# Chunked attention by pairs of heads in 64-row matmuls, on one core

## The chip, the cores and the metric

The kernel runs on one core of one Trainium2 chip. A core has TensorE (matmuls, written PE in the profile, its weight loads PEld), VectorE (DVE), ScalarE (ACT), GpSimd (POOL) and SyncE (SP), which starts most transfers. Matmuls write into PSUM, eight banks of 512 float32 columns in each of 128 partitions; VectorE and ScalarE read from there. The metric is the device time of one execution in microseconds (us); lower is better.

## The reference

One layer of a streaming encoder over 1024 positions of 1024 features, in float32. Cut to what matters here:

```python
def chunk_attention(q, k, v, rel_bias):      # 8 heads of 64
    # chunks of 64 positions; each attends to its own and the 8 chunks before
    ...
        s = einsum('bqhd,bkhd->bhqk', qb, kb) * scale + bias
        s = where(valid, s, -inf)
        pr = softmax(s, axis=-1)
        return einsum('bhqk,bkhd->bqhd', pr, vb)

def reference(x, p, ...):
    hn = rmsnorm(h, norm_mix_g)
    z = hn @ w_in
    u = z[..., :512]                          # four pooling groups
    q, k, v = split(z[..., 512:], 3)
    a = pool_mixer(u, pool_w, pool_b, pool_scale)
    o = chunk_attention(q, k, v, rel_bias)
    h = h + concatenate([a, o]) @ w_out
    # then a gated MLP with a causal convolution, a gated input embedding, a final norm
    ...
```

## The kernel before

Every large product is made in three matmuls (`mm3`): both operands are split into a high part and a remainder (`split`: a rounding copy on ScalarE, a subtraction on VectorE), and high by high, high by low and low by high are added in PSUM. A step of 128 contraction rows and 512 columns is thus three matmuls of 512 columns.

The stages follow each other: load x and start the first head pair's q and k and the first half of v; attention, with the rest of the input projection dealt out among it; the pooling mixer and the output projection; the MLP; the gate and the final norm. TensorE's order is the order in which the program issues (`manual_schedule`); the other engines are ordered by a scheduler with priorities (`high_priority`) and dependences.

Attention works by tiles of 128 queries. Query tile t needs the key tiles t-4 to t, so 1, 2, 3, 4 or 5 key tiles (`key_tiles`); the eight query tiles of a head need 1, 2, 3, 4, 5, 5, 5, 5. The loop visits i = 0 to 63, eight query tiles for each of eight heads, one head after the other. In a visit:

- `scores(i)`: the operands of a head are stacked in 128 rows (`qk_stack`): `Q1` holds q high over q low, `K2` and `K1` hold k so that two full-row matmuls make all products of high and low parts. Scores go to banks 4 and 5. Then VectorE adds the bias and takes the row maximum (as a minimum of the negated scores) in one instruction (line 354 for five key tiles, 362 for fewer), ScalarE makes the exponential with its row sum (364), VectorE the reciprocal (365), and ScalarE (every third visit, 367) or VectorE (369) scales.
- filling: `credit` steps of the remaining input projection (`rest`, made of `project` and `project_v`), in banks 0 and 1. `fill_room` deals `FILL` steps out over the visits.
- in the middle of the filling, `probs_t(i - 2)`: 128 by 128 transposes (378) of the probabilities of two visits ago into banks 6 and 7, with the high copy (385) and the low part (386) into `PT`.
- at every second visit `values`: the products with V (395, 396), 256 queries at a time, in bank 2 or 3, and their sum over the high and low columns (401, 402) into `o32`.

There are three buffers `Sb` of probabilities and two of bias. Evacuations of filling products are on lines 272 (q and k), 268 (v) and 454 (pooling groups).

Of the kernel before, what the change touches and what calls it, by code (L numbers as in the profile page):

```python
# [11 lines left out]
P = 128  # L12
# [52 lines left out]
FILL = 164  # L65
BASE = 2.0
LATER = 3
DRAIN = 4
# [4 lines left out]
def key_tiles(i):  # L73

    return min(i % NTOK + 1, BANDT) if 0 <= i < N_HEADS * NTOK else 0


def fill_room():


    vec_t, pe_t = [], []
    for i in range(N_HEADS * NTOK):
        a, b = key_tiles(i), key_tiles(i - 2)
        vec_t.append(BASE + 0.2 * key_tiles(i - 3) + 0.13 * b)
        pe_t.append(0.11 * a + 0.11 * b + (0.22 * (key_tiles(i - 5) + 1) if i % 2 and i >= 5 else 0.0))
    lo, hi = 0.0, 10.0
    for _ in range(60):
        m = (lo + hi) / 2
        room = [max(0.0, m * v - p) / 0.65 for v, p in zip(vec_t, pe_t)]
        lo, hi = (m, hi) if sum(room) < FILL else (lo, m)  # L90
    return room


def trunk(tc, xT, pT, vecs, w_qk0, w_in, w_v, bias, counts, pool_w, w_out, w_up, w_down,
# [4 lines left out]
    with tc.tile_pool(name="sb", bufs=1) as sb, \  # L99
# [47 lines left out]
        st = [small[:, 56 + 3 * i:59 + 3 * i] for i in range(3)]  # L147
        sa = [small[:, b:b + 3] for b in (24, 27, 30, 33, 66, 69)]
# [7 lines left out]
        stacks = []  # L156
        for s in range(2):
            base = r(96 + 12 * s, 3072).rearrange("p (a t) -> p a t", a=3)
            stacks.append((base[:, 0], base[:, 1], base[:, 2]))
# [6 lines left out]
        biasb = [f(12 + 2.5 * s, 640) for s in range(2)]  # L166
        Sb = [f(b, 640) for b in (17, 19.5, 57.5)]
# [106 lines left out]
        def qk_stack(j):  # L274

            Q1, K1, K2 = stacks[j]
            a = slice(HD * j, HD * j + HD)
            b = slice(HD * (1 - j), HD * (1 - j) + HD)
            q, k = qk32[0], qk32[1]
            todo = []  # L280
            for h in range(2):
                z = slice(h * 512, (h + 1) * 512)
                todo += [
                    lambda z=z: act.activation(Q1[a, z], q[a, z], AF.Copy, scale=-0.125),
                    lambda z=z: dve.scalar_tensor_tensor(Q1[b, z], q[a, z], -0.125, rv(Q1[a, z]),
                                                         ALU.mult, ALU.subtract),
                    lambda z=z: act.activation(K2[a, z], k[a, z], AF.Copy),
                    lambda z=z: dve.tensor_tensor(K2[b, z], k[a, z], rv(K2[a, z]), ALU.subtract),
                    lambda z=z: act.activation(K1[b, z], k[a, z], AF.Copy),
                    lambda z=z: dve.tensor_copy(K1[a, z], rv(K2[b, z])),  # L290
                ]
            return todo
# [27 lines left out]
        later += qk_stack(0)  # L320
        run_later(len(later))
        later += qk_stack(1)
# [6 lines left out]
        def load_bias(h):  # L329
            b = biasb[h % 2]  # L330
# [5 lines left out]
        def keys(i):  # L336
            t = i % NTOK
            k0 = max(0, t - 4)
            return i // NTOK, t, k0, t + 1 - k0

        def scores(i):
            h, t, k0, nk = keys(i)
            Q1, K1, K2 = stacks[h % 2]
            b = biasb[h % 2]
            q = Q1[:, t * P:(t + 1) * P]
            S = Sb[i % 3]
            s_ = st[i % 3]
            n, ki = nk * P, k0 * P
            if nk == BANDT:
                for z in range(2):  # L350
                    ks = slice(ki + 320 * z, ki + 320 * z + 320)
                    pe.matmul(PS[:, 4 + z, 0:320], q, K2[:, ks], start=True, stop=False)  # L352
                    pe.matmul(PS[:, 4 + z, 0:320], q, K1[:, ks], start=False, stop=True)  # L353
                dve.tensor_tensor_reduce(
                    S.rearrange("p (a b) -> p a b", a=2), PS[:, 4:6, 0:320],
                    b.rearrange("p (a b) -> p a b", a=2), 1.0, BIG, ALU.add, ALU.min, s_[:, 0:1])
            else:
                nn = max(n, 256)
                z = 4 + t % 2
                pe.matmul(PS[:, z, 0:nn], q, K2[:, ki:ki + nn], start=True, stop=False)  # L360
                pe.matmul(PS[:, z, 0:nn], q, K1[:, ki:ki + nn], start=False, stop=True)  # L361
                dve.tensor_tensor_reduce(S[:, 0:n], PS[:, z, 0:n], b[:, 640 - n:640],  # L362
                                         1.0, BIG, ALU.add, ALU.min, s_[:, 0:1])
            act.activation(S[:, 0:n], S[:, 0:n], AF.Exp, bias=s_[:, 0:1], scale=-1.0, accum_out=s_[:, 1:2])  # L364
            dve.reciprocal(s_[:, 2:3], s_[:, 1:2])
            if i % 3 == 0:
                act.activation(S[:, 0:n], S[:, 0:n], AF.Copy, scale=s_[:, 2:3])
            else:
                dve.tensor_scalar(S[:, 0:n], S[:, 0:n], s_[:, 2:3], None, ALU.mult)

        def probs_t(i):
            h, t, k0, nk = keys(i)
            S = Sb[i % 3]
            w = i // 2
            pt = PT[w % 2]
            pst = PS[:, 6:8].rearrange("p a b -> p (a b)")[:, 0:nk * P]
            for j in range(nk):
                pe.transpose(pst[:, j * P:(j + 1) * P], S[:, j * P:(j + 1) * P], ident)  # L378
            pst = pst.rearrange("p (k q) -> p k q", k=nk)
            i0 = k0 - (t // 2 * 2 - 4)  # L380
            qs = slice(t % 2 * P, (t % 2 + 1) * P)
            hi = pt[:, 0, i0:i0 + nk, qs]
            lo = pt[:, 1, i0:i0 + nk, qs]
            with tc.high_priority(AHEAD):
                act.activation(hi, pst, AF.Copy)
                dve.tensor_tensor(lo, pst, rv(hi), ALU.subtract)

        def values(wi):
            h, w = wi // 4, wi % 4
            pt = PT[wi % 2]  # L390
            ks = list(range(max(0, 2 * w - 4), 2 * w + 2))
            O = PS[:, 2 + wi % 2, 0:256]
            for n_, k in enumerate(ks):
                idx = k - (2 * w - 4)
                pe.matmul(O, V[:, k, h], pt[:, 0, idx], start=n_ == 0, stop=False)  # L395
                pe.matmul(O, V[:, k, h], pt[:, 1, idx], start=False, stop=n_ == len(ks) - 1)  # L396
            j = h % 2
            a = slice(HD * j, HD * j + HD)
            c = slice(HD * (1 - j), HD * (1 - j) + HD)
            with tc.high_priority(AHEAD):  # L400
                act.activation(otmp[a], O[c], AF.Copy)
                dve.tensor_tensor(o32[a, h // 2, w * 256:(w + 1) * 256], O[a], otmp[a], ALU.add)

        nw = [0]
        bankn = [0]

        def project(ct, evac, heads=0, eng=dve):
            hi, lo = wring[nw[0] % 2]
# [913 lines left out]
```

## Time and profile before

| What | us |
|---|---|
| median of 3 runs (lowest, highest) | 1135.18 (1134.28, 1135.48) |
| profiled execution | 1134.33 |
| its span in the trace | 1132.6 |
| TensorE busy in the span | 1123.2 |
| VectorE busy | 889.3 |
| ScalarE busy | 600.6 |
| attention stage, from the first scores to the last values | 54 to 274 |

The profile is of one execution. A row of the group view gives line, engine, operation, output and inputs, shapes and count, then busy time, the mean of one in ns, and the idle time before the group with what ended it. The timeline gives start, length, engine and line. Matmuls overlap, and the length of one is partly modelled; the distance from one start to the next says what it costs TensorE. In the view of stretches the columns are the length, then each engine's busy time with its number of instructions, the granted TensorE clock (1.00 is full), the DMA share and the rate. A row of the waits says who waited for whom, for how long in all, how often, and the longest.

### The profile page before, as it was taken

To read this page: it belongs to the slowest core of one execution; us is meant where nothing else is said; L and a number is where in the kernel's file an instruction comes from. 1 tells how busy PE (TensorE), PEld (TensorE's weight loads), DVE (VectorE), ACT (ScalarE), POOL (GpSimd) and SP (SyncE) were. 2 spreads that over 40 slices of the span, in tenths; PEclk is the share of its full clock that TensorE was granted. 3 is DMA by queue.
4 is the path that set the end of the run, shared out by engine and by line. 5 is a ranking of instruction groups with operands and counts; after the bars stand their busy time and mean duration, and the time that the engine had idled before them with its cause. 6 is when DMAs were issued, how large, how long until landed. Compare 5 with 4: busy or idle time off the path is not lost.

```text
span 1132.6 us, 15484 instructions
## 1 busy us (share of the span) xinstructions
PE 1123.2 (99%) x5554; PEld 948.4 (84%) x5554; DVE 889.3 (79%) x1532; ACT 600.6 (53%) x1056; POOL 143.1 (13%) x188
## 2 busy tenths in 40 slices
PE   9999999999999999999999999999999999999997
PEld 7988998888888888888888888888888888888887
DVE  8678878879658888887788788877877789986845
ACT  8568677765654554444444344444444435564634
POOL 0000000074002210120112011201120112000000
PEclk9999999999999999999999999999999999999999
DMA  7010102104500154575557555765576556420003
GB/s 268 38 49 31 50 12 69 40 29 137 189 19 10 61 148 135 142 174 141 145 153 176 140 143 152 162 157 132 152 160 158 144 149 128 151 93 19 1 27 122
DMA packets 64588, 124.81 MB, mean 110 GB/s; under 512 B 7296, under 2 KB 8704, under 8 KB 64512
## 3 DMA queue, kind: packets, MB, share of 16 engines
q1 hardware_dynamic: 50400, 98.33, 25.9%
q0 software_dynamic: 13824, 25.17, 13.9%
q8 instruction: 43, 0.70, 0.2%
q10 hardware_dynamic: 288, 0.33, 0.1%
q14 instruction: 33, 0.27, 0.1%
HBM read 109.13 MB, written 14.68 MB: 109 GB/s over the span
## 4 chain that ended last, share of the span: by engine, by line
PE 91%; DVE 4%; ACT 2%; issue 1%; POOL 1%; DMA 0%; SPq 0%; POOLq 0%; DVEq 0%; ACTq 0%
PE PS L128 28%; PE PS L129 28%; PE PS L130 28%; PE PS L378 2%; PE PS L396 1%; PE PS L395 1%; DVE R L134 1%; PE PS L353 1%; PE PS L352 1%; ACT R L133 0%; PE PS L361 0%; PE PS L360 0%; ACT F L364 0%; DMA F<-in_xT 0%; POOL TB L786 0%
## 5 line engine op out<-in xcount | busy, mean ns | idle before, releaser
L128 PE MATMUL PS<-R 128*128 128x512 f32 (+1 forms) x1136 | 435.1, 383 | 0.0
L130 PE MATMUL PS<-R 128*128 128x512 f32 (+1 forms) x1136 | 430.6, 379 | 0.0
L129 PE MATMUL PS<-R 128*128 128x512 f32 (+1 forms) x1072 | 412.7, 385 | 0.2 <-DVE R L241 0.2
L130 PEld LDWEIGHTS PS<-R 128*128 128x128 f32 x1136 | 213.5, 188 | 40.7
L128 PEld LDWEIGHTS PS<-R 128*128 128x128 f32 x1136 | 213.7, 188 | 38.8 <-ACT R L133 0.5
L133 ACT ACTIVATE R<-F 128x512 fp32r<-128x512 f32 (+2 forms) x225 | 140.6, 637 | 176.2 <-PE PS L129 77.9
L129 PEld LDWEIGHTS PS<-R 128*128 128x128 f32 x1072 | 201.6, 188 | 38.5 <-DVE R L241 1.3
L134 DVE TENSOR_TENSOR R<-F,R 128x512 fp32r<-128x512 f32 (+2 forms) x221 | 152.3, 700 | 46.7 <-ACT R L133 45.5
L1021 DVE TENSOR_TENSOR F<-F,PS 128x512 f32<-128x512 f32 x140 | 92.6, 681 | 6.8 <-PE PS L130 6.6
L133 ACT ACTIVATE BQ<-RW 128x512 fp32r<-128x512 f32 x90 | 52.6, 622 | 81.6 <-PE PS L129 77.6
L711 DVE TENSOR_TENSOR F<-F 128x512 f32<-128x512 f32 x88 | 60.5, 688 | 37.4 <-DMA F<-in_w_up 36.1
L964 POOL DMA_DIRECT2D RW<-Yd x56 | 49.1, 878 | 255.4 <-DMA RW<-Yd 194.5
L964 POOL DMA_DIRECT2D RW<-in_w_down x40 | 35.5, 949 | 236.3 <-DMA RW<-in_w_down 193.9
L134 DVE TENSOR_TENSOR BQ<-RW,BQ 128x512 fp32r<-128x512 f32 x90 | 59.1, 684 | 2.9 <-PE PS L129 2.2
L364 ACT ACTIVATE F<-F,small 128x640 f32<-128x640 f32 (+2 forms) x64 | 44.4, 693 | 21.5 <-DVE small L362 13.4
L129 PE MATMUL PS<-BQ 128*128 128x512 f32 x140 | 54.6, 390 | 0.1
L130 PE MATMUL PS<-BQ 128*128 128x512 f32 x140 | 54.5, 389 | 0.0
L128 PE MATMUL PS<-R,BQ 128*128 128x512 f32 x140 | 54.5, 389 | 0.0
L129 PE MATMUL PS<-R,BQ 128*128 128x512 f32 x140 | 54.5, 389 | 0.0
L130 PE MATMUL PS<-R,BQ 128*128 128x512 f32 x140 | 54.5, 389 | 0.0
L128 PE MATMUL PS<-BQ 128*128 128x512 f32 x140 | 54.5, 389 | 0.0
L847 ACT ACTIVATE F<-F,vec 128x1024 f32<-128x1024 f32 (+1 forms) x25 | 28.6, 1143 | 43.5 <-DVE F L822 37.2
(188 smaller groups left out, 1797.7 us busy)
## 6 DMA issues: line engine op xcount, KB each, us to landing
F<-in_w_up SPq DMA_DIRECT2D x91, 256.0 KB, 3.8
RW<-Yd SPq DMA_DIRECT2D x60, 256.0 KB, 3.6
RW<-Yd POOLq DMA_DIRECT2D x56, 256.0 KB, 4.7
RW<-in_w_down SPq DMA_DIRECT2D x50, 256.0 KB, 2.9
RW<-in_w_down POOLq DMA_DIRECT2D x40, 256.0 KB, 6.2
Yd<-F SPq DMA_DIRECT2D x40, 256.0 KB, 3.5
F<-in_w_in SPq DMA_DIRECT2D x10, 512.0 KB, 3.5
F<-in_xT SPq DMA_DIRECT2D x16, 256.0 KB, 5.8
```

The lines of the kernel that those rows point to most:

```text
L128: pe.matmul(ps, ahi, bhi, start=first, stop=False, skip_group_check=more)
L129: pe.matmul(ps, ahi, blo, start=False, stop=False, skip_group_check=more)
L130: pe.matmul(ps, alo, bhi, start=False, stop=last, skip_group_check=more)
L133: both = (act.activation(hi, src, AF.Copy), dve.tensor_tensor(lo, src, rv(hi), ALU.subtract))
L134: dve.tensor_tensor(lo, src, rv(hi), ALU.subtract))
L352: pe.matmul(PS[:, 4 + z, 0:320], q, K2[:, ks], start=True, stop=False)
L364: act.activation(S[:, 0:n], S[:, 0:n], AF.Exp, bias=s_[:, 0:1], scale=-1.0, accum_out=s_[:, 1:2])
L378: pe.transpose(pst[:, j * P:(j + 1) * P], S[:, j * P:(j + 1) * P], ident)
L711: return dve.tensor_tensor(rawu[to], rawu[a], rawu[b], op)
L847: act.activation(y, Gb[:, 2 + a:2 + b], AF.Identity, bias=vec[:, C_CB + fi:C_CB + fi + 1], scale=cw(2))
L964: pool.dma_start(t, src, accum_op=ALU.add)
L1021: dve.tensor_tensor(t, t, PS[:, 4 + d], ALU.subtract if n in (1, 5) else ALU.add)
```

## The change

Two heads are handled together, each in 64 of TensorE's 128 rows. A *unit* is a pair of heads and a query tile (the two shortest tiles, 0 and 1, make one unit): 28 units, seven for each of four pairs, take the place of 64 visits.

- Operands: q high, q low, k high and k low of the pair lie in tiles of their own, the first head in rows 0 to 63 and the second in rows 64 to 127 (`lay` takes the place of `qk_stack`, with copies of 128 rows). q has one buffer and k two.
- `scores(u)`: three products of 64 rows per key range (high by high, high by low, low by high), alternating between the two heads; the heads write different banks of 4 to 7.
- `probs_t(u - 1)`: each 128 by 128 block is transposed in two halves of 64 rows and 64 columns, which alternate between row halves and write two banks. They are issued first in unit u, right ahead of its scores, so that all 64-row work of a unit is together. For units of five key tiles the first three key tiles go to columns 320 and on of banks 4 to 7, the others to banks 2 and 3.
- `probs_out`: the high copies and low parts, now in two pieces of three and up to two key tiles; `softmax`: as before, with the first head scaled on VectorE and the second on ScalarE. There are two `Sb`, one for each head, and three bias buffers.
- After that the filling steps of the unit, and last `values(u - 1)`, if its tile is odd, for both heads, into the one of banks 0 and 1 that the filling product in progress does not use; if that product has only begun, filling goes on first.
- Filling: `fill_room` has other costs and deals out 168 steps by the new lengths; `project` loads and splits the next block's weights while the present block runs; k comes ahead of q, and `lay_due` says when each half of them may be laid.

```diff
-FILL = 164
-BASE = 2.0
-LATER = 3
-DRAIN = 4
+FILL = 168
+BASE = 6.0
+LATER = 8
+DRAIN = 9
...
+UNITS = [(c, ts) for c in range(N_HEADS // 2) for ts in [(0, 1)] + [(t,) for t in range(2, NTOK)]]
...
+    for u in range(NU):
+        vec_t.append(BASE + 0.2 * (key_tiles(u) + key_tiles(u - 1)) + 0.25 * window_keys(u - 1))
+        pe_t.append(0.4 + 0.18 * key_tiles(u) + 0.11 * key_tiles(u - 1) + 0.48 * window_keys(u - 1))
...
-        room = [max(0.0, m * v - p) / 0.65 for v, p in zip(vec_t, pe_t)]
+        room = [max(0.0, m * v - p) / 0.68 for v, p in zip(vec_t, pe_t)]
...
+        Q = [r(96 + 4 * x, 1024) for x in range(2)]
+        K = [[r(104 + 8 * s + 4 * x, 1024) for x in range(2)] for s in range(2)]
...
+        def scores(u):
...
+                wide = n // 2 if nk > 3 else max(n, 256)
+                places = [[4 + x + 2 * (z + y) for y in range(2 if nk > 3 else 1)] for x in range(2)]
+                for i, (q, k) in enumerate(((Q[0], Kh), (Q[0], Kl), (Q[1], Kh))):
+                    for y in range(len(places[0])):
+                        for x in range(2):
+                            pe.matmul(PS[:, places[x][y], 0:wide], q[halves[x], t * P:(t + 1) * P],
+                                      k[halves[x], ki + y * wide:ki + (y + 1) * wide], start=i == 0, stop=i == 2,
+                                      tile_position=(HD * x, 0))
...
+        def probs_t(u):
...
+                return (4 + 2 * x, 320 + HD * m) if m < 3 else (2, P * x + HD * (m - 3))
...
+                    for y in range(2):
+                        pe.transpose(PS[:, bank + y, col:col + HD], Sb[x][halves[y], m * P:(m + 1) * P],
+                                     ident[halves[y], halves[y]], tile_position=(HD * y, 0))
...
+        def values(u):
...
+            while c_ >= 2 and len(v_ready) < 2 * w + 2 or u < NU - 1 and at[0] < 2:
+                next(fill)
+                credit -= 1
...
+                O = PS[:, (bankn[0] + 1) % 2, 256 * j:256 * j + 256]
...
+        for u in range(NU + 1):
...
+            turned_ = probs_t(u - 1) if u else []
+            sums = scores(u) if u < NU else []
+            probs_out(turned_)
+            for todo in sums:
+                softmax(*todo)
+            if u < NU:
...
+                credit += room[u]
+                while credit >= 1 and next(fill, True) is not False:
+                    credit -= 1
+                    lay_due(u)
+                run_later(LATER)
+                if u:
+                    values(u - 1)
+        for _ in range(DRAIN):
+            next(fill)
+        values(NU - 1)
```

More of the change, by code (lines that the diff above doesn't have):

```diff
@@ L146, in trunk @@
         rstd_tok = small[:, 8:16]
[L147 to L148 removed]
+        st = [small[:, b:b + 3] for b in (24, 27, 30, 33, 56, 59, 62, 66)]
         cnt = small[:, 40:56]
@@ L334, in load_bias, with softmax @@
             pool.memset(b[64:128, 0:64], BIG)
[L336 to L353, printed above, removed]
+        def softmax(x, b, ps, S, s_):
+            n = S.shape[-1]
+            if len(ps.shape) == 3:
@@ L371, in probs_t @@
[L371 to L386, printed above, removed]
@@ L388, in values @@
-        def values(wi):
-            h, w = wi // 4, wi % 4
-            pt = PT[wi % 2]
-            ks = list(range(max(0, 2 * w - 4), 2 * w + 2))
[L392 to L402, printed above, removed]
+            if x:
+                act.activation(S, S, AF.Copy, scale=s_[:, 2:3])
+            else:
+                dve.tensor_scalar(S, S, s_[:, 2:3], None, ALU.mult)
```

225 lines of the change are left out of this document (127 added, 98 removed).

## The prediction

> **What bounds the kernel now.** I read the page first.
>
> ```profile
> span 1132.6 us, 15484 instructions
> PE 1123.2 (99%) x5554; PEld 948.4 (84%) x5554; DVE 889.3 (79%) x1532; ACT 600.6 (53%) x1056; POOL 143.1 (13%) x188
> PE 91%; DVE 4%; ACT 2%; issue 1%; POOL 1%; DMA 0%; SPq 0%; POOLq 0%; DVEq 0%; ACTq 0%
> ```
>
> TensorE is busy all the time and carries the chain that ended last. The change touches only the attention stage, from the first scores at 54 us to the last values at 274 us, so next came the stretch view and the waits of that stage.
>
> ```profile
> core 0: us, PE busy (x) PEld busy (x) DVE busy (x) ACT busy (x) POOL busy (x), PEclk, DMA share, GB/s
> 54.00:274.00 220.00, 219.03 (x1367) 193.93 (x1366) 177.76 (x433) 153.38 (x328) 34.91 (x62) 1.00 0.14 46
> ```
>
> ```profile
> PE PS L378 <- DVE B L386: 0.8, 2, 0.5
> ```
>
> TensorE idles 1.0 us of 220 and its only named wait in the stage is 0.8 us, at a full granted clock. So the stage is as long as its sum of matmul slots. VectorE is busy 177.8 us (81%): if TensorE gets less work, VectorE's order is next. A busy share does not give slots, since matmuls overlap; slots are the distances between starts in the timeline.
>
> ```profile
> 201.14 0.30 PE L352 MATMUL PS<-R 128*128 128x320 f32 x1
> 201.28 0.31 PE L353 MATMUL PS<-R 128*128 128x320 f32 x1
> 201.42 0.31 PE L352 MATMUL PS<-R 128*128 128x320 f32 x1
> 201.57 0.31 PE L353 MATMUL PS<-R 128*128 128x320 f32 x1
> 201.72 0.39 PE L128 MATMUL PS<-R,B 128*128 128x512 f32 x1
> ```
>
> ```profile
> 263.03 0.39 PE L130 MATMUL PS<-R 128*128 128x512 f32 x1
> 263.26 0.71 PE L378 MATMUL PS<-ident,F 128*128 128x128 f32 x5
> 263.72 0.48 PE L128 MATMUL PS<-R 128*128 128x512 f32 x1
> 264.04 0.39 PE L129 MATMUL PS<-R 128*128 128x512 f32 x1
> ...
> 268.50 0.28 PE L395 MATMUL PS<-B,R 128*128 128x256 f32 x1
> 268.61 0.28 PE L396 MATMUL PS<-B,R 128*128 128x256 f32 x1
> ```
>
> A score product of 320 columns takes a slot of 0.145 us (0.58 over four), one of 512 columns 0.23, one of 256 columns 0.12; 384 columns lie between, 0.175. Five transposes with what they push back: from 263.26 to the next product's start, less its 0.23 slot (264.04 - 0.23 = 263.81), 0.55, so 0.11 each. A filling step (three products of 512) takes 0.69.
>
> **Part 1: scores.** Before, a head and query tile multiplies stacked 128-row operands: two products per key range. A head has four tiles of five key tiles (four slots of 320 columns) and tiles of 1, 2, 3, 4 key tiles (two slots of 256, 256, 384, 512): 16 x 0.145 + 4 x 0.12 + 2 x 0.175 + 2 x 0.23 = 3.61 us, for eight heads 28.9. After, three products of 64 rows per range, for two heads in two row halves. If two halves run side by side, a pair of heads has 24 slots of 0.145, 6 + 6 of 0.12 and 3 of 0.175: 5.45 us, for four pairs 21.8. That removes 7.1. One after the other they take 43.6 and add 14.7. No instruction of this trace uses part of the rows, so this is the first open price. I take side by side: the halves read different rows and write different banks.
>
> **Part 2: transposes.** 240 of 0.11 make 26.4 us; the count is in this row.
>
> ```profile
> L378 PE MATMUL PS<-ident,F 128*128 128x128 f32 x240 | 37.1, 274 | 1.0 <-DVE B L386 0.8
> L395 PE MATMUL PS<-B,R 128*128 128x256 f32 x144 | 36.1, 284 | 0.0
> ...
> L378 PEld LDWEIGHTS PS<-ident,F 128*128 128x128 f32 x240 | 28.8, 140 | 9.8 <-DVE B L386 4.3
> L395 PEld LDWEIGHTS PS<-B,R 128*128 128x128 f32 x144 | 27.2, 189 | 1.0
> ```
>
> After, there are 480 of 64 rows and 64 columns, in 240 pairs. Does a pair take half of 0.11? A 128-column transpose lasts as long as a 256-column product (274 and 284 ns) while its weight load is shorter (140 against 189): it looks bound by its columns, and half of them take half. Then 13.2 us remain, 13.2 less. Against it stand products with a single column, which still take 0.10 each:
>
> ```profile
> 334.82 0.79 PE PS L628 x8
> 335.61 0.35 PE PS L128
> ```
>
> If loading the weights sets the slot, a pair takes 0.11 still and nothing is gained; if the halves follow each other, 480 x 0.11 = 52.8, 26.4 more. I take the half, being nearest to the transposes' own rows.
>
> **Part 3: entering and leaving 64-row work.** 28 units (seven per pair of heads) each go in and out once. Going from product to transposes costs nothing today (0.23 from 263.03 to 263.26), so the low end is 0. The high end is a full stop: the tail of a product beyond its slot, 0.39 - 0.23 = 0.16, plus a load of 0.19, so 0.35 each, 19.6 in all. I take 0.2 each, the middle, 0.4 per unit: 11.2 us.
>
> The Trainium skill, "TensorEngine Tiling (Array Packing)", Key Properties, speaks against the change here: changing the tiling mode, not merely the tile, drains TensorE. It gives no price; by it the low end falls away, and the sum below keeps its 11.2.
>
> Values stay at the 288 matmuls of before (two rows of 144): 0. They now write the bank that the next filling product wants, which must wait for two copies and two adds:
>
> ```profile
> L402 DVE TENSOR_TENSOR F<-PS,F 64x256 f32<-64x256 f32 x31 | 13.0, 419 | 2.3 <-ACT F L401 1.9
> ...
> L401 ACT ACTIVATE F<-PS 64x256 f32<-64x256 f32 x31 | 11.7, 378 | 7.9 <-PE PS L396 7.4
> ```
>
> That is 2 x 0.80 = 1.6, behind the next unit's transposes, scores and switches (1.8): 0, and 1.6 for the one window in eight that ends with a product if that cover is late. Fewer, wider splits of q and k, a third bias buffer (one more DMA at the start, ahead of the first filling weights, while value tiles still run) and weights split earlier relieve engines that do not bound: 0. Filling work is the same, only dealt out anew.
>
> **Part 4: the softmax loop.** Before, probabilities are transposed two visits after their scores, in the middle of filling work. After, a unit's transposes stand first in the next unit, and TensorE, being in order, holds all filling products behind them. The loop from transposes to transposes for a unit of five key tiles:
>
> ```profile
> L386 DVE TENSOR_TENSOR B<-PS,B 128x384 fp32r<-128x384 f32 x8 | 4.4, 554 | 1.9 <-ACT B L385 1.7
> L386 DVE TENSOR_TENSOR B<-PS,B 128x256 fp32r<-128x256 f32 x8 | 3.4, 423 | 0.2
> L354 DVE CUSTOM_DVE_ANT_0 F<-PS,F 128x640 f32<-128x640 f32 x32 | 26.1, 816 | 2.6 <-PE PS L353 2.3
> L369 DVE TENSOR_SCALAR F<-F,small 128x640 f32<-128x640 f32 x21 | 12.2, 583 | 0.5
> L365 DVE RECIPROCAL small<-small 128x1 f32<-128x1 f32 x64 | 10.3, 161 | 16.5 <-ACT F L364 16.1
> L272 DVE TENSOR_TENSOR F<-PS,F 128x512 f32<-128x512 f32 x12 | 8.2, 685 | 0.6 <-PE PS L130 0.5
> ```
>
> ```profile
> L385 ACT ACTIVATE B<-PS 128x384 fp32r<-128x384 f32 x8 | 3.9, 485 | 4.7 <-PE PS L378 4.7
> L364 ACT ACTIVATE F<-F,small 128x640 f32<-128x640 f32 x32 | 26.5, 827 | 7.7 <-DVE small L354 6.7 <-DVE small L365 0.9
> L364 ACT ACTIVATION_READ_ACCUMULATOR F<-F,small 128x1 f32 x64 | 12.0, 187 | 0.0
> L367 ACT ACTIVATE F<-F,small 128x640 f32<-128x640 f32 x11 | 9.0, 821 | 0.5 <-DVE small L365 0.5
> ```
>
> Time 0 is the end of the transposes. Scores take 6 x 0.145 + 0.16 = 1.03. The high copies of the first three key tiles lie in the scores' banks and I let them wait: ScalarE has them done at 1.5 and 2.0 (0.485 each). VectorE's low parts (0.55, 0.55, 0.42) end at 3.0, the two additions with bias (0.82 and 0.9 with its accumulator's read) at 3.9 and 4.8. ScalarE's exponentials (0.83 + 0.19) end at 4.95 and 6.0, the second reciprocal at 6.2, its scaling on ScalarE (0.82) at 7.0; five pairs of transposes (0.055) close the loop at 7.3, with handovers 7.4.
>
> TensorE's own work in a unit: transposes 0.55, scores 0.87, switches 0.4, filling by `fill_room` as the diff gives it (7.0 steps at query tiles 5 and 7, 5.3 at tile 4, 4.6 at tile 6, of 0.69), values 16 or 24 x 0.12 at tiles 4 and 6. That is 6.65 at tiles 5 and 7, 7.4 at tile 4, 7.9 at tile 6. So tiles 5 and 7 wait 0.75 each, 8 units, 6.0 us. Units with fewer key tiles have shorter loops and wait nothing.
>
> **Sum.** -7.1 - 13.2 + 11.2 + 6.0, and the 1.0 us of today's idle: -4.1. The profiled execution took 1134.33 us (span 1132.6), 0.85 below the median of 1135.18; from the median, 1131.1.
>
> **The rivals.**
>
> *Copies need not wait* for scores in the same bank: then they run under the scores, the loop is about 1 us shorter, tiles 5 and 7 wait nothing, and the sum is -10.1: 1125; with switches at half price -15.7: 1119.5. In today's trace transposes (banks 6 and 7) and scores (4 and 5) lie apart, so it tells nothing. The Trainium skill, "PSUM — Partial Sum Buffer", section on bank collisions, says two engines must be kept apart in a bank even at different columns; by it this rival falls.
>
> *Other vector work inside the loop* (the other side). VectorE also evacuates filling products (0.685, L272) and splits weights; these are 0.685 long and cannot be interrupted. One such step inside the loop of each unit of five key tiles adds 0.69 at tiles 5, 7 and 4 (12 units) and 0.2 at tile 6 (4): 9.1, a sum of +5.0: 1140. It decides from 0.35 us per unit on (4.1 over 12 units). For it: VectorE is 81% busy and had two visits of slack, now one unit. Against: VectorE has 1 us free at the loop's end, and qk splits shrink.
>
> *Pairs overlap only in part.* Transposes bound by loads: 13.2 lost, tiles 5 and 7 then wait 0.5: +7.1, so 1142. With score slots at 0.19 too, 6.6 more: 1149. The Trainium skill, "TensorE: Matmul & The Clock Gate", measured speedup, has 3.07 of an ideal 4 for four row tiles; no run here shows it.
>
> *The halves do not run side by side*: +14.7 + 26.4 + 11.2 - 1.0 = 51: 1186. Nothing in the trace speaks for it but the missing evidence.
>
> *Nothing changes*: price and gain cancel within 0.2% (2.3 us, about what a measurement of this kernel can tell from no change).
>
> **How the numbers follow.** Forecast case 0.45 (0.30 faster, 0.10 the same, 0.05 slower, as switches cost 0.15 or 0.3), copies free 0.13, vector work in the loop 0.22, partial overlap 0.10, no overlap 0.06, cancelling 0.04. Faster 0.43, same 0.14, slower 0.43. The range leaves out no overlap, the far part of partial overlap and a little at the low end: 1120 to 1147; the forecast's own range is 1127 to 1136.
>
> **What would show it.** Score pairs 0.145 us apart, not 0.29; transposes in pairs 0.055 apart, not 0.11; a gap of about 0.2 us at each change between 64-row and 128-row work; TensorE waiting for the scaling of the second head at the units of tiles 5 and 7 by some 0.75 us, 6 us in the stage. The prediction is wrong if these waits exceed 10 us, or if no slot shrinks.

## The result and the profile after

| | us, median | ratio to before, 95% interval |
|---|---|---|
| before | 1135.12 | |
| with the change | 1162.65 (1162.09 to 1164.92) | 1.0247 [1.023, 1.0265] |

The change makes the kernel 27.5 us slower: the forecast of 1131.1 missed, on the other side and outside its range of 1120 to 1147. The first lines and the chain that ended last, from the page of the kernel after:

```profile
span 1160.8 us, 16207 instructions
PE 1123.4 (97%) x5914; PEld 938.6 (81%) x5914; DVE 868.7 (75%) x1530; ACT 591.6 (51%) x1074; POOL 144.2 (12%) x188
PE 82%; DVE 8%; ACT 5%; issue 2%; DMA 1%; POOL 1%; SPq 0%; POOLq 0%; DVEq 0%; ACTq 0%
```

The span grew by 28.2 us and VectorE's share of the chain from 4 to 8%. Where: the view of stretches, attention first and then all that follows; and TensorE's waits in the first stretch.

```profile
54.00:315.00 261.00, 232.22 (x1786) 195.00 (x1784) 175.78 (x462) 154.75 (x364) 35.51 (x60) 0.99 0.14 48
315.00:1160.00 845.00, 838.78 (x3812) 697.49 (x3810) 657.24 (x1010) 401.89 (x653) 105.20 (x112) 1.00 0.46 122
```

```profile
PE PS L433 <- DVE F L438: 20.0, 16, 2.2
PE PS L395 <- ACT F L351: 4.2, 8, 1.2
PE PS L433 <- DVE R L275: 1.7, 2, 1.0
PE PS L395 <- DVE F L353: 1.7, 4, 0.8
```

TensorE idles 28.8 of the 261 us (before, 1.0 of 220). Nothing is lost after the stage: its last 845 us hold 838.78 us of TensorE work, the amount of before. The first row is the largest part of the answer: 16 times, the products of probabilities with V (line 433) wait for an addition on VectorE (line 438), 20.0 us in all. The transposes (395) wait 5.9 us for the scaling of the softmax, close to the 6.0 of the forecast; seven of the eight waits for the second head's scaling (351) stand behind units of tiles 5 and 7, as forecast. The groups of TensorE's instructions say the same, in their last column:

```profile
L433 PE MATMUL PS<-B,R 128*128 128x256 f32 x144 | 38.8, 302 | 21.8 <-DVE F L438 20.0 <-DVE R L275 1.7
L395 PE MATMUL PS<-ident,F 64*128 64x64 f32 x480 | 22.7, 231 | 5.8 <-ACT F L351 4.2 <-DVE F L353 1.7
```

One such place in the timeline, of TensorE, then of ScalarE and VectorE:

```profile
199.25 0.28 PE L434 MATMUL PS<-B,R 128*128 128x256 f32 x1
200.45 0.39 PE L433 MATMUL PS<-B,R 128*128 128x256 f32 x1 [0.92 <-DVE F L438]
```

```profile
199.57 0.38 ACT L437 ACTIVATE F<-PS 64x256 f32<-64x256 f32 x1
```

```profile
198.66 0.69 DVE L291 TENSOR_TENSOR R<-F,R 128x512 fp32r<-128x512 f32 x1
199.27 0.55 DVE L353 TENSOR_SCALAR F<-F,small 128x640 f32<-128x640 f32 x1
199.73 0.16 DVE L349 RECIPROCAL small<-small 128x1 f32<-128x1 f32 x1
199.98 0.42 DVE L438 TENSOR_TENSOR F<-PS,F 64x256 f32<-64x256 f32 x1
```

The first head's last product starts at 199.25. Its copy (437) and its addition (438) read the left half of a bank; the second head's first product writes the right half of the same bank. It starts at 200.45, right after the addition, instead of at 199.37. The code issues copy and addition inside the loop over the two heads, ahead of the second head's products, and the dependence goes by banks. The Trainium skill, "PSUM — Partial Sum Buffer", section "PSUM bank collisions raise a hardware error", says that a second engine must stay out of a bank even at other columns, on the same 32 partitions; the trace agrees in so far as the program waits in each of the 16 windows.

A long wait can cost a second time, as this view of stretches shows for the one that ends at 114.7 us:

```profile
112.00:114.60 2.60, 0.50 (x5) 0.29 (x3) 1.51 (x4) 2.52 (x6) 0.00 (x0) 0.98 0.00 0
114.60:118.00 3.40, 3.27 (x20) 3.05 (x22) 0.07 (x1) 0.31 (x1) 0.00 (x0) 0.51 0.00 0
118.00:121.00 3.00, 3.00 (x26) 2.37 (x23) 2.61 (x9) 1.63 (x6) 0.00 (x0) 1.00 0.00 0
```

For 3.4 us the granted clock is 0.51, and the value products take slots of 0.21 us in place of 0.12. The same follows the wait of 1.68 us that ends at 184.8 (granted clock 0.50 from 186.2 to 189.6), but not the one of 2.20 us that ends at 276.5 (1.00 from 276.6 to 280.0). Two such stretches, 6.8 us at half clock, cost some 3.4 us.

### The profile page after: what moved, and what is told of

The parts are those of the page before. It is cut to its first block, busy times and chain, and to the rows that moved or that the text cites. A ratio compares the mean times of both kernels' runs of the same rounds, so it can differ in the third digit from the quotient of the medians.

```text
span 1160.8 us, 16207 instructions
## 1 busy us (share of the span) xinstructions
PE 1123.4 (97%) x5914; PEld 938.6 (81%) x5914; DVE 868.7 (75%) x1530; ACT 591.6 (51%) x1074; POOL 144.2 (12%) x188
## 4 chain that ended last, share of the span: by engine, by line
PE 82%; DVE 8%; ACT 5%; issue 2%; DMA 1%; POOL 1%; SPq 0%; POOLq 0%; DVEq 0%; ACTq 0%
PE PS L138 26%; PE PS L139 26%; PE PS L140 25%; DVE B L414 2%; PE PS L433 2%; DVE R L144 2%; PE PS L434 1%; PE PS L395 1%; DVE F L343 1%; ACT B L413 1%; ACT F L348 1%; PE PS L370 1%; ACT R L143 1%; DVE F L438 1%; ACT F L351 1%
## 5 line engine op out<-in xcount | busy, mean ns | idle before, releaser
L143 ACT ACTIVATE R<-F 128x512 fp32r<-128x512 f32 (+2 forms) x235 | 147.2, 637 | 179.0 <-PE PS L139 74.0
L144 DVE TENSOR_TENSOR R<-F,R 128x512 fp32r<-128x512 f32 (+2 forms) x231 | 159.8, 702 | 50.9 <-ACT R L143 44.4
L414 DVE TENSOR_TENSOR B<-PS,B 128x384 fp32r<-128x384 f32 (+2 forms) x104 | 45.1, 463 | 28.7 <-ACT B L413 27.8
L433 PE MATMUL PS<-B,R 128*128 128x256 f32 x144 | 38.8, 302 | 21.8 <-DVE F L438 20.0
L348 ACT ACTIVATE F<-F,small 128x640 f32<-128x640 f32 (+4 forms) x64 | 44.1, 691 | 28.7 <-DVE small L343 23.1
L140 PE MATMUL PS<-R,BQ 128*128 128x512 f32 x140 | 54.5, 389 | 0.0
L139 PE MATMUL PS<-R,BQ 128*128 128x512 f32 x140 | 54.5, 389 | 0.0
```

Source lines behind the costliest of these rows:

```text
L139: pe.matmul(ps, ahi, blo, start=False, stop=False, skip_group_check=more)
L140: pe.matmul(ps, alo, bhi, start=False, stop=last, skip_group_check=more)
L143: both = (act.activation(hi, src, AF.Copy), dve.tensor_tensor(lo, src, rv(hi), ALU.subtract))
L144: dve.tensor_tensor(lo, src, rv(hi), ALU.subtract))
L348: act.activation(S, S, AF.Exp, bias=s_[:, 0:1], scale=-1.0, accum_out=s_[:, 1:2])
L414: dve.tensor_tensor(lo, src, rv(hi), ALU.subtract)
```

## The experiments

Times are medians against the kernel before on the same chip (1135.0 to 1135.8 in all of them). Waits are TensorE's between 54 and 315 us. Line numbers are those of each run's own kernel: the transposes stand in 395 or 398, a filling step begins at 138, the additions that empty the values' bank are 438, 440 or 443.

| Run | us | ratio, 95% interval |
|---|---|---|
| e4, rows in turn | 1169.4 | 1.0308 [1.0293, 1.0324] |
| e2, two banks | 1152.4 | 1.0157 [1.0141, 1.0173] |
| e1, copies after both heads | 1146.8 | 1.0113 [1.0094, 1.0132] |
| e5, e1 and filling dealt anew | 1152.2 | 1.0147 [1.013, 1.0164] |
| e9, e1 without the second scaling | 1140.2 | 1.0042 [1.0025, 1.0059] |
| e6, e1 and softmax first | 1145.6 | 1.009 [1.0075, 1.0105] |
| e7, e1 and values early in a product | 1157.8 | 1.0189 [1.0161, 1.0217] |
| e8, e6 with e7 | 1155.5 | 1.0169 [1.0147, 1.0191] |
| e10, e6 with the loop cut | 1144.0 | 1.0072 [1.0055, 1.0089] |
| e11, e6 levelled | 1145.2 | 1.0085 [1.007, 1.01] |
| e12, e11 and scaling on VectorE | 1144.4 | 1.0078 [1.006, 1.0096] |
| e13, e12 and copies first | 1144.9 | 1.0092 [1.0066, 1.0118] |
| e14, e10 without the values' copies | 1134.7 | 0.9994 [0.9985, 1.0004] |
| e15, e1 two units deep | 1141.0 | 1.0052 [1.0038, 1.0066] |
| e19, e1 and values in banks of their own | 1142.2 | 1.0062 [1.005, 1.0075] |
| e16, e15 with e19 | 1130.2 | 0.9959 [0.9947, 0.9972] |
| e17, e16 and softmax first | 1130.5 | 0.9958 [0.9946, 0.9971] |
| e18, e16 with whole transposes | 1133.9 | 0.9991 [0.9982, 1.0] |

### The values' bank, and the row halves

**e1_out_after** issues both heads' products before either head is copied out.

```diff
-                with tc.high_priority(AHEAD):
-                    act.activation(otmp[a], O[c], AF.Copy)
-                    ...
+                outs_.append((O, halves[j], halves[1 - j]))
+            for O, a, c in outs_:
+                with tc.high_priority(AHEAD):
+                    act.activation(otmp[a], O[c], AF.Copy)
+                    ...
```

> The changed kernel with one edit: in a window of values the products of both heads are issued first, and the two copies and additions that empty their bank after both. Theory (one bank): the second head's products wait in 16 windows for VectorE's addition of the first head, since both heads write halves of one bank; 22.8 us of TensorE's idle time in the changed kernel stand there, 1.08 at the least in each window. Then that wait is gone; the shorter units give some 3 us back to the wait for the softmax, so 1143, 1140 to 1148. Rival (late vectors): the second head would wait anyway, for probabilities or for VectorE's turn; the wait moves and the time stays at 1160 to 1163. Rival (64-row price): most of the loss is in changes of mode and pairs that overlap in part; the wait goes but the time falls by under 8 us, to 1155 or more.

1146.8: 15.9 us less, as expected. The wait between the heads is gone. Its waits:

```profile
PE PS L395 <- ACT F L351: 4.9, 8, 1.0
PE PS L138 <- DVE F L440: 4.1, 4, 2.0
PE PS L395 <- DVE F L353: 3.5, 5, 1.0
```

The transposes now wait 8.4 us, since the stops between the heads no longer give the softmax time, and the next filling product (138) waits 4.1 for the values' bank.

**e2_two_banks** leaves the copies where they were and gives each head a bank (`O = PS[:, 2 + j, 256:512]`).

> The changed kernel with one edit: the first head's values go to columns 256 to 511 of bank 2 and the second head's to those of bank 3, in place of the two halves of the free filling bank; the copies and additions stay behind each head's products. Theory (one bank): the second head no longer waits (0 of 16 windows against 16), but the next unit's transposes, which write banks 2 and 3 for key tiles 4 and 5 and in short units, now wait for the additions, about 1 us in most of 14 windows; 1150, 1145 to 1157. Rival (late vectors): the second head waits as before and the time is 1160 or more.

1152.4. The second head waits no more, but the next unit's transposes do, for the same addition, since they write those banks:

```profile
PE PS L395 <- DVE F L438: 13.4, 23, 1.1
```

Both runs show the shared bank, emptied between the two heads, to be the cause of most of the loss; e2 shows that another bank alone hands the wait on.

**e4_rows_in_turn** issues all scores of one head, then all of the other (`for x in range(2)` as the outer loop), as a test of the row halves in the kernel after.

> The changed kernel with one edit: the score products of a query tile are issued head by head (all of the first 64 rows, then all of the second), not alternating. Theory (pairs run side by side because they alternate): slots of 0.145 us each, not two in one; 12 in place of 6 in a unit of five key tiles, 0.87 us more in 16 units, 0.36 to 0.72 in 12, so 20 us of TensorE work, of which units that wait for the softmax or the bank hide up to 7: 1176, 1170 to 1184. Rival (64-row price): the pairs barely overlap now, so the order does not matter: 1160 to 1166.

1169.4, 6.7 more than the change: below the expected 1170 to 1184 and above the rival's 1166. The halves overlap in part even so. The kernel after first, then e4, in the timeline: transposes, twelve score products, the next product:

```profile
159.98 1.13 PE L370 MATMUL PS<-R 64*128 64x320 f32 x12
161.03 0.39 PE L138 MATMUL PS<-R 128*128 128x256 f32 x1
```

```profile
162.09 1.52 PE L370 MATMUL PS<-R 64*128 64x320 f32 x12
163.55 0.39 PE L138 MATMUL PS<-R 128*128 128x256 f32 x1
```

From the first score to the product 1.05 us became 1.46; with no overlap it would have been near 1.9. That two halves run side by side is shown.

### The waits that are left, one at a time

All of these start from e1.

**e9_no_second_scale** leaves out the scaling of the second head (`if not x:`, only the first scaled), so every second head's output is not normalised.

> The first run's kernel (both heads' products, then the copies) without the scaling of the second head's probabilities by its reciprocal: that ScalarE instruction of 0.81 us (five key tiles) is left out, so the values of every second head are not normalised. TensorE's work is the same. Theory (softmax loop): in eight units TensorE waits 1.2 us for the second head's scaling, 9.4 us in all; the loop gets 0.8 to 0.9 us shorter where it binds, so 5 to 7 us of that wait go: 1140.5, 1139 to 1143. Rival (vector engines' sum of work): ScalarE is at 51% of the span and has time to spare, so leaving out 20 us of its work changes nothing: 1145 to 1148.

1140.2, as expected. The wait at the transposes fell from 8.4 to 3.3, so the softmax's length is what they wait for.

**e5_new_deal** deals the filling by the measured loop lengths and holds values back only right at a product's first step.

```diff
-        vec_t.append(BASE + 0.2 * (key_tiles(u) + key_tiles(u - 1)) + 0.25 * window_keys(u - 1))
+        vec_t.append({0: 7.3, 2: 5.1, 3: 6.0}.get(UNITS[u][1][0], 7.6))
...
-            ... or u < NU - 1 and at[0] < 2:
+            ... or u < NU - 1 and at[0] < 1:
```

> The edit of the first run (both heads' products, then the copies) with the filling steps dealt out anew: unit lengths proportional to 7.6 us for five key tiles, 6.0 for four, 5.1 for three, 7.3 for the unit of two tiles, in place of the formula, and values held back only while the filling product in progress is in its first step, not its first two. Theory (softmax loop of 7.4 us): TensorE's waits at the transposes, 6.7 us in the changed kernel, shrink to 2 or 3; 1136 to 1141, 3 to 5 under the first run. Rival (late vectors): the vector engines set the pace whatever the deal; within 2 us of the first run.

1152.2, a miss. The transposes wait 4.4 instead of 8.4, but one wait for the values' bank is 6.4 us long: VectorE stood behind an operation of the next stage that waited 6.3 us for GpSimd, and ScalarE behind one that waited 6.8.

```profile
PE PS L138 <- DVE F L440: 6.4, 1, 6.4
```

**e6_softmax_first** puts the softmax under `high_priority(AHEAD)`. **e7_values_early** lets values only start while the filling product is at its steps 2 to 5 (`not 2 <= at[0] <= 5`). **e8_all_three** has both and keeps V one tile further ahead (`len(v_ready) < min(2 * w + 3, NTOK)`).

> The first run's kernel with the softmax instructions given the same raised priority as the copies behind transposes and products, so that weight splits, splits of q and k and evacuations are not put among them. Theory (softmax loop with other vector work in it): in a binding unit two foreign VectorE instructions of 0.68 us stand inside the loop (an evacuation of q, a split); with most of them behind it the wait at the transposes falls from 9.4 to about 4 us: 1142, 1139 to 1145. Rival (the loop is its own chain): foreign work only fills its gaps; within 2 us of 1146.8.

> The first run's kernel, with values let in only while the filling product in progress is in its steps 2 to 5 (before: from 2 on), so that at least two filling steps (1.4 us) lie between the values and the next product, which wants their bank. Theory (one bank, second half): the first run's four waits of products for VectorE's addition of values, 4.1 us, go; the added filling steps shift some 2 us to the units after: 1144, 1142 to 1146. Rival: the waits are those of a late VectorE and reappear elsewhere: 1146 to 1149.

> The edits of the two runs before it together, and values of the third and fourth pair held back until one more tile of V is done than they need (2.0 us of waits for the last part of V in the first run). By the theories 9.4 falls to 4, 4.1 and 2.0 to under 1: 1138, 1135 to 1142. If the vector engines only shift their delay, 1144 or more.

e6 gave 1.2 us, which its runs (1143.9 to 1147.2) hardly tell from e1's (1146.1 to 1150.8), though the transposes' waits fell from 8.4 to 5.5. e7 lost 11 against e1 and e8 10 against e6: the wait for the bank fell from 4.1 to 0.9, but the steps taken early to reach the right place were missing in the next unit, which is one of the long ones (of tile 7's filling 3 steps were left in the unit at 213.2, against 7 in e1's at 207.3). e7's waits:

```profile
PE PS L395 <- DVE F L353: 9.5, 7, 2.9
PE PS L395 <- ACT F L351: 5.9, 9, 1.2
```

Much of the loss is the clock: behind waits of 2.2, 2.9 and 1.7 us, e7's profile has 17.1 us at a granted clock of 0.50, some 8.5 us of work lost, where e1's has 3.4 us (1.7).

**e11_level** takes e6 and moves 0.8 steps from tiles 2 and 3 to 5 and 7; **e12_level_dve** scales the second head on VectorE besides; **e13_empty_first** raises the values' copies to `high_priority(4 * AHEAD)` as well.

> The kernel of raised softmax priority with 0.8 filling steps more in the units of query tiles 5 and 7 and 0.8 less in those of tiles 2 and 3, nothing else dealt anew. Theory (softmax loop): tiles 5 and 7 wait some 0.7 us each and have 0.55 more work now; tiles 2 and 3 have shorter loops and wait nothing: waits at the transposes from 6.3 to 3, so 1142.5, 1141 to 1145. Rival (late vectors): no change within 1.5 us, or slower as in the new deal.

> The levelled kernel with the second head's probabilities scaled on VectorE like the first's (0.58 us in place of 0.82 on ScalarE, and one handover less). Theory (softmax loop): the loop is 0.3 to 0.5 us shorter where it binds: 1 to 3 us under the levelled kernel: 1140.5, 1139 to 1143. Rival (VectorE's sum of work): VectorE gets 15 us more and delays evacuations: equal or slower than the levelled kernel.

> The levelled kernel with both heads scaled on VectorE, and the copies and additions that empty the values' bank raised four times as far in priority (240 instructions ahead, not 60). Theory (one bank, second half): the filling product that follows waits for that bank because VectorE does splits and evacuations first (3.9 us in three waits, the longest 1.9); put ahead of them, 3 us of it go, part of it returning at the transposes: 1142.5, 1140 to 1144. Rival (VectorE's sum of work): the work put behind is waited for elsewhere: 1144 or more.

All three lie within 1.2 us of e6. What the transposes saved came back at other buffers (weights' low parts: 2.6 us in e11), and e13's wait for the bank stayed 3.8 us. The raised priority moved nothing: in the whole program every engine runs the same instructions in the same order as in e12. So e13 is e12 once more and says nothing of its theory.

**e10_loop_cut** takes e6 and lets the transposes read constants that are ready long before (`rstd_bc[...]` in place of `Sb[x][...]`), so its attention output is not the reference's; **e14_no_waits** also leaves out the values' copies and additions.

> The kernel of raised softmax priority with the loop cut: the transposes read a constant tile (the row factors) in place of the probabilities, so no transpose waits for a softmax; the softmax is still computed, its result is unused and the attention output is not the reference's. All engines do the same instructions. Theory (64-row work itself saves about 6 us of TensorE's work, waits take it back): the waits at the transposes (6.3 us) go and nothing takes their place: 1139, 1137 to 1141, above the kernel before by the waits left (products for their bank 4.1, V 2.2, a split 1.2) less the 6. Rival (64-row price): the matmuls themselves cost more than before, and the time stays at 1143 or more.

> The kernel with the loop cut, and without the copies and additions that empty the values' bank (all but the last); the attention output is set to zero once in their place, so nothing of the computed attention reaches the result. TensorE's instructions are all there. Theory (64-row work itself is cheaper for TensorE, by about 7 us as read from the slots, and waits take that back): with the waits for the softmax and for the values' bank both gone, 5 to 6 us of other waits left (V, a split of weights), the time falls below the kernel before: 1131, 1128 to 1134. Rival (64-row price): the 64-row work is no cheaper, and without these waits the time comes down only to that of the kernel before or above: 1135 to 1140.

e10 is the miss that taught most. No transposes wait, yet 1144.0:

```profile
PE PS L138 <- DVE F L440: 7.3, 4, 3.5
```

The wait moved to the bank, 4.1 to 7.3. With that gone too (e14), the time is that of the kernel before, above the expected 1131. Its stops (counted as in the next section) are still 7.9 us longer than before's, 2.4 of them ahead of the stage and 2.2 behind it, and they use up what the matmul work gains.

### Both waits taken out by distance

**e15_two_deep** takes e1 and transposes a unit's probabilities two units after its scores; two more buffers lie in parts of `o32`, `U` and the third bias buffer while these are unused. **e19_own_banks** takes e1 with its transposes one unit behind, and moves the values into the middle of the unit's filling and into columns 256 to 511 of banks 2 and 3. **e16_deep_own_banks** does both, **e17_deep_first** adds e6's priority.

```diff
-            turned_ = probs_t(u - 1) if u else []
+            turned_ = probs_t(u - 2) if u > 1 else []
...
+                half = credit / 2 if u > 1 else 0
+                if u > 1:
+                    while credit >= max(1, half) and next(fill, True) is not False:
+                        credit -= 1
+                        lay_due(u)
+                    values(u - 2)
...
-                O = PS[:, (bankn[0] + 1) % 2, 256 * j:256 * j + 256]
+                O = PS[:, 2 + j, 256:512]
```

In e15 to e17 the scores of the next pair's tile 2 overwrite one block of tile 7's transposed probabilities before it is copied, so that block's part of the output is another. **e18_deep_clean** puts tile 7's blocks of the first head into banks 2 and 3 (`return 2, HD * m`) and one buffer elsewhere, and computes the whole reference.

> The pair's two products ahead of both copies, as in e1_out_after, and besides a unit's probabilities are transposed two units after its scores (four probability buffers in place of two), so that the softmax has a whole unit's filling work to finish in. Theory (the softmax loop and the bank of the values are the two waits that are left, and they are separate): TensorE waits 0 for the softmax at the transposes (8.4 us in e1_out_after), 4 to 7 us for the values' bank stay, 1139 us (1137 to 1142). Rival (VectorE's order moves the waits, as when the loop was cut by reading constants): 1144 or more, with over 8 us at the bank.

> e1_out_after with the values in the middle of the unit's filling steps and in columns 256 to 511 of banks 2 and 3, but with transposes one unit after their scores as in the change: the other single step between e1_out_after and e18_deep_clean. Theory (two separate waits): the filling products' wait for the values' bank (4.1 us) goes, the transposes' wait for the softmax (8.4 us) stays: 1141 us (1138 to 1143). Rival (the waits feed each other through VectorE's order): the transposes wait 11 us or more and the time stays above 1144.

> e15_two_deep with the values in the middle of the unit's filling steps and in columns 256 to 511 of banks 2 and 3, which no filling product uses. Theory: neither the transposes nor the filling products wait, only V's second part (2 to 3 us) and 1 us of weights are left, and the slots' gain shows: 48.2 us of 64-row work and its switches in place of 55.3, so -7.1, and +3 of waits beyond today's: 1131 us (1128 to 1133). Rival (VectorE, not the two waits, holds the stage: the waits reappear at other buffers): 1136 to 1142.

> e16_deep_own_banks with the softmax at the higher priority of e6_softmax_first. Theory (with a unit of slack the softmax's place in VectorE's order no longer matters): within 1.5 us of e16_deep_own_banks. Rival (the split copies and V's evacuation, held back behind the softmax, come late): 2 to 5 us longer, with waits for weights or V.

> e16_deep_own_banks with the transposes of query tile 7 in columns that the scores of the next pair's tile 2 do not write (in e16 those scores overwrote one block of them before it was copied), and one probability buffer elsewhere for one unit; so the whole reference is computed. Theory (nothing in the order of work depends on those columns): within 1.5 us of e16_deep_own_banks, 1130 us (1129 to 1132), faster than the kernel before by 0.4%. Rival (the overwritten block freed TensorE of a wait that now returns): 1133 to 1137, with a wait at the scores or transposes of tile 2.

Alone, two units of distance bring 5.8 us and the values' own banks 4.6; together 16.6 in e16, and 12.9 in e18, which computes the whole reference. So the waits feed each other, by 2.5 to 6.2 us. Both times lie in their theories' ranges, but not the waits: in e15 the transposes still wait, now for the additions of the scores whose banks they share, and in e19 they wait 4.1 us for the values' addition besides, since the values now lie in banks that the transposes write:

```profile
PE PS L398 <- DVE small L346: 3.6, 7, 0.9
PE PS L138 <- DVE F L443: 3.3, 2, 2.1
```

```profile
PE PS L395 <- ACT F L351: 4.3, 8, 1.0
PE PS L395 <- DVE F L440: 4.1, 4, 1.8
```

e16 hit its expectation (1131, measured 1130.2), and e17 shows that with a unit of slack the softmax's priority is worth nothing. e16's longest waits:

```profile
PE PS L398 <- DVE F L443: 0.9, 2, 0.6
PE PS L437 <- DVE B L417: 0.8, 1, 0.8
```

e18 came 3.7 us behind e16, in its rival's range but not with the rival's wait (at tile 2's scores or transposes): 28.8 us below the change, and not told from the kernel before (its interval reaches 1.0). The difference is one row, values that wait for the low parts of tile 7's probabilities, in the three short units of tile 2 that follow a tile 7, where the middle of the filling comes early, and once after the last unit:

```profile
PE PS L441 <- DVE B L421: 3.5, 4, 1.5
```

VectorE's order in e18 shows why: both additions of scores (350) now stand between the low parts (421), where in e16 they came behind all four. Values at the end of those units were not tried.

```profile
108.80 1.02 DVE L421 TENSOR_TENSOR B<-PS,B 128x384 fp32r<-128x384 f32 x2 [0.98 <-ACT B L420]
109.73 0.55 DVE L350 CUSTOM_DVE_ANT_0 F<-PS,F 128x384 f32<-128x384 f32 x1
110.36 0.42 DVE L421 TENSOR_TENSOR B<-PS,B 128x256 fp32r<-128x256 f32 x1
110.70 0.55 DVE L350 CUSTOM_DVE_ANT_0 F<-PS,F 128x384 f32<-128x384 f32 x1
...
111.83 0.42 DVE L421 TENSOR_TENSOR B<-PS,B 128x256 fp32r<-128x256 f32 x1
```

## Why the prediction was wrong

**The step that failed is in Part 3: values at 0.** It took the values' last copies and additions (2 x 0.80) as a matter for the next *filling product*, and found cover for that. The next user of the bank is the second head's own products, which follow the first head's at once, with no cover at all. By the prediction's own rows a copy and an addition are 0.80 per window, 12.8 over 16 windows; the trace has 20.0, since both copy and addition also stand behind what their engines are doing (up to 2.2 us). The kernel showed it: the copies lie inside the loop over the heads. With that term the sum would have been about 1144 to 1151, slower. e1 took it away and gained 15.9 us.

**Part 4, the softmax loop: mechanism right, term too small.** Predicted 6.0 us of waits, measured 5.9 in the kernel after, but 8.4 in e1, where no stops between the heads lend the softmax time; so the agreement of 5.9 with 6.0 is luck. The loop that was worked out at 7.4 took 8.2 there. TensorE's rows, transposes to transposes, and VectorE's between them, in e1:

```profile
206.45 0.28 PE L435 MATMUL PS<-B,R 128*128 128x256 f32 x1
206.66 0.84 PE L395 MATMUL PS<-ident,F 64*128 64x64 f32 x20
207.31 1.13 PE L370 MATMUL PS<-R 64*128 64x320 f32 x12
208.36 0.50 PE L138 MATMUL PS<-R,B 128*128 128x512 f32 x1
208.70 0.39 PE L139 MATMUL PS<-R,B 128*128 128x512 f32 x1
...
215.19 0.53 PE L395 MATMUL PS<-ident,F 64*128 64x64 f32 x10 [0.47 <-ACT F L351]
215.52 0.71 PE L370 MATMUL PS<-R 64*128 64x256 f32 x8
```

```profile
208.04 0.43 DVE L440 TENSOR_TENSOR F<-PS,F 64x256 f32<-64x256 f32 x1 [0.44 <-ACT F L439]
...
210.70 0.68 DVE L279 TENSOR_TENSOR F<-PS,F 128x512 f32<-128x512 f32 x1
...
212.78 0.69 DVE L294 SCALAR_TENSOR_TENSOR R<-F,R 128x512 fp32r<-128x512 f32 x1
```

From 207.31 to 215.52 is 8.2. The values' additions of the unit before (440) and two steps of other vector work (279, 294) stand inside it: the second rival, which had put that work at 0.69 a unit and a time of 1140. It was there, though it was not what turned the sign; putting the softmax ahead of it (e6) took 2.9 us off the transposes' waits and 1.2 off the time.

**Parts 1 to 3, the matmul work: right in kind, 2 us too good.** The rows above hold the switch: transposes 0.21 after the last value product where 0.12 is its slot, and 0.34 from the first product to the next in place of 0.23. From 206.45 to the second product at 208.70 are 2.25 us; less the slots of a value product (0.12), of a filling product (0.23), of ten pairs of transposes and of six pairs of scores, 0.41 is left per unit (predicted 0.4). A pair of scores takes 0.146 (predicted 0.145), a pair of transposes 0.061 (predicted 0.055). To get the net gain I add up over a whole trace how far the distances between starts exceed their slots; of a run of transposes or 64-row products, with the changes at its ends, I count what exceeds about the shortest run of its kind. Spans and stops are of the same profiled execution:

| | span, us | stops, us | span less stops |
|---|---|---|---|
| before | 1132.6 | 7.5 | 1125.1 |
| with the change | 1160.8 | 43.1 | 1117.7 |
| e14 | 1133.2 | 15.4 | 1117.8 |
| e16 | 1127.6 | 9.4 | 1118.2 |
| e18 | 1131.0 | 12.9 | 1118.1 |

So the matmul work shrank by 6.9 to 7.4, where -7.1 - 13.2 + 11.2 had given 9.1. Some 1.4 of the 2 are the transposes (240 x 0.006), about 0.3 the switches (28 x 0.01) and 0.4 a 29th visit, for the last unit's transposes alone.

**The other rivals.** Partial overlap and halves one after the other fell with the pitches and e4. That copies need not wait for scores in the same bank was not tested by a run of its own, but the kernel after speaks against it: in all 12 units of tiles 5 to 7 the two copies of three key tiles, which lie in the scores' banks, start after the scores' end (scores 159.98 to 161.10, copies at 161.89 and 162.26), while the first copy out of banks 2 and 3 starts at 160.21. The prediction's own marks did not catch the miss: the waits for the scaling stayed under 10 us and the slots shrank as said; the wait that cost most was none of those that it named.

**The sum as measured**, in spans: -7.4 of matmul work and +35.6 of stops, 28.2. Of the stops 27.8 are TensorE's idle time in the stage (28.8 against 1.0) and some 3.4 the two stretches at half clock; the other 4 or so lie around the stops, where 1.20 us from start to start, as at 200.45, are 1.08 beyond the slot and only 0.92 of them count as idle.

## What to carry to other kernels

When two accumulations share a bank, look for the *next* instruction that writes that bank, not for the one that the bank was reserved for: issuing both before either is read out was worth 15.9 us here. Where a loop over several engines held TensorE up here, removing one wait mostly moved it to the next buffer that the same VectorE serves; one more unit of distance together with a bank of its own was worth more than both apart (16.6 us, or 12.9 in the kernel that computes everything, against 5.8 and 4.6). A saving in matmul slots is worth having only if the waits that the new order adds stay below it: 7 us of gain stood against 36 us of stops.

## What the runs showed of the hardware

- Products in the two row halves overlap in part even when all of one half are issued ahead of the other: twelve in 1.46 us (e4), against 1.05 when they alternate.
- A wait of about 2 us can be enough to halve the granted clock for 3.4 us. In e1 (granted clock 0.50 from 263.8 to 267.2):

```profile
263.23 0.50 PE L138 MATMUL PS<-R 128*128 128x512 f32 x1 [2.02 <-DVE F L440]
263.57 0.43 PE L139 MATMUL PS<-R 128*128 128x512 f32 x1
263.80 0.62 PE L140 MATMUL PS<-R 128*128 128x512 f32 x1
264.22 0.63 PE L138 MATMUL PS<-R 128*128 128x512 f32 x1
```

After 2.02 us of waiting, the slot goes from 0.23 to 0.42. The length of the wait alone does not decide: in the kernel after, one of 1.68 us had this sequel and one of 2.20 had not, in e11 one of 2.58 had not (clock 1.00 from 179.4 to 182.8), and in e2 two close ones of 0.43 and 0.89 had it. What decides stays open. The Trainium skill, "TensorE: Matmul & The Clock Gate", section "Why this matters for your kernels", advises to avoid idle gaps of more than about 3 us; here shorter ones did it at times.
- A visit to 64-row work costs about 0.41 us in switching, all told (e1, from 206.45 to 208.70).
